# Attention branch: U of the seven-product quads summed ahead, and a fourth such quad in its first pass

## The chip, the cores and the metric

The kernel runs on one core of one Trainium2 chip. The metric is the device time of one execution in microseconds (us), lower is better. A core has a matrix engine (TensorE, "PE"; its weight loads are "PEld"), a vector engine (VectorE, "DVE"), a scalar engine (ScalarE, "ACT"), GpSimd ("POOL") and SyncE ("SP"), which here issues nearly all DMAs. Each engine works through its own instructions in a fixed order; semaphores make them wait for one another.

## The reference

One layer of a hybrid block, batch 1, 256 tokens, width 2048, fp32: causal attention with ALiBi and three dilated patterns (16 heads of 128), a chunked state-space scan (inner width 4096, 8 groups), two sigmoid gates, an output product and norms. Cut to the part around the change:

```python
hn = rms_norm(x, norm_w)
proj = hn @ w_in          # q, k, v, z_a, z_s, xbc, dt, g_a, g_s
...
o_a = o_a.reshape(b, s, ATTN_WIDTH) * jax.nn.silu(z_a)
...
merged = jax.nn.sigmoid(g_a) * (o_a @ w_attn_branch) + jax.nn.sigmoid(g_s) * (y @ w_ssm_branch)
return x + merged @ w_out
```

The change is in `o_a @ w_attn_branch`: 256x2048 by 2048x2048.

## The kernel before

**Precision.** Every fp32 operand is split in a high part h (an ACT copy to the fast fp32 format) and a low part l (a DVE subtract, operand minus h). A product is a "triple" of three matmuls, each 128x128 by 128x512: x-high by h, x-high by l, x-low by h (L484 to L486).

**Stages.** first, dt, the groups B, C, xs, zs (with gs between), then ssm, v, the 16 heads (q, k, za for each), ga, attn, out. All weights lie packed in DRAM as `wall`, tiles of 128x1024 (512 KB), numbered in the order of use: a *unit* is one such tile. attn's first pass has the tiles 417 to 432 and its second 433 to 448. A plain tile is loaded in a ring "w" of 5 places and split to h and l (L278, L279), rings of 4 places each.

**gemm_pair.** ssm, v, ga, attn and out are computed in two passes, c = 0 and c = 2, each over two blocks of 512 columns and both blocks of 128 rows: four accumulators `ps_<stage><c>_0..3`. A pass goes over *quads* of two k-tiles (two weight tiles). In a plain quad all eight products are computed: 24 matmuls. The quads in S_QUADS use a seven-product scheme (Strassen's in Winograd's form): 21 matmuls, with four more accumulators `pp_<stage><c>_0..3`. With the weights as A = (B11, B21), tile n, and (B12, B22), tile n+1, it needs T = (B12 − B11, B22 − B12 + B11), U = A minus T's second half T2, and C = B22. All of A, C, T, U are split: ha/la, hc/lc, htt/ltt, htu/ltu (ACT L551, DVE L552); U is a DVE subtract of 128x1024 (L565), made in place in `wa`. The left sides `sx` are made before. The T and U pairs share two places, ht/lt.

After a pass, *fold* (two ACT copies L589 and L590, four DVE adds L591 to L594) puts the product sums together; in attn, *attend* adds each accumulator (L1154), and *merge* (L1143, L1144) applies the gate to `th_a` and adds to `th_s`. In pass c = 2 accumulators and product banks swap the PSUM banks that they have in c = 0.

**Sums ahead.** For the quads in SUMS_SSM and SUMS_ATT, T is made in an earlier stage, where DVE has time: *sum_jobs* hangs on a unit a `get`, which loads tile n+1 whole and the left half of tile n, and three units later an `add`: two DVE subtracts of 128x512 (L254, L255), then the T is written to DRAM ("spill", L242). A POOL copy of one column (L249, L253) ties each place to the unit. gemm_pair then fetches T (L533) and C (L534) and makes no T. The 21 jobs for ga, attn and out run in the heads' stage, one every 15/4 units, in the space that `th_a` takes up later. In attn, T and C go to `fin`.

**What sets the order.** SP issues loads in the order of the code, each after its place is free. On PE, DVE and ACT a scheduler sets a fixed order when the program is built, by its own estimates of time and the priorities in the code (`high_priority`); the order of quads is written by hand in A_ORDERS.

Of the kernel before, what the change touches and what calls it, by code (L numbers as in the profile page):

```python
# [9 lines left out]
F32 = mybir.dt.float32  # L10
F32R = mybir.dt.float32r
AF = mybir.ActivationFunctionType
ALU = mybir.AluOpType
PSUM = bass.MemoryType.PSUM

P = 128
# [8 lines left out]
UNIT = 1024  # L25
# [12 lines left out]
GT_LAGS = (3, 5, 6), (2, 3, 4)  # L38
Y_AFTER = 0, 0
GS_BEFORE = {0: (0, 1), 4: (2,)}  # L40
A_ORDERS = {0: (0, 1, 2, 4, 3, 6, 5, 7), 2: (0, 2, 1, 4, 3, 5, 6, 7)}
V_ORDERS = {0: (0, 2, 4, 1, 3, 5, 6, 7), 2: (0, 2, 1, 4, 3, 5, 6, 7)}
G_ORDERS = {c: (0, 2, 4, 1, 3, 5, 6, 7) for c in (0, 2)}
O_LEFT = {0: {0: (0, 3), 4: (1, 5)}, 2: {}}
# [5 lines left out]
S_QUADS = {  # L50
    ("ssm", 0): (5, 7, 8, 10, 11, 12, 13), ("ssm", 2): (3, 5, 7, 8, 10, 11, 12, 13),
    ("v", 0): (2, 3, 4, 5, 6), ("v", 2): (2, 4, 5, 6), ("ga", 0): (2, 3, 4, 5, 6), ("ga", 2): (2, 3, 4, 5, 6),
    ("attn", 0): (2, 4, 6), ("attn", 2): (2, 4, 5, 6), ("out", 0): (3, 5), ("out", 2): (3, 5),
}
Y_ORDERS = {0: (0, 1, 2, 3, 5, 4, 7, 8, 6, 10, 11, 9, 12, 14, 13, 15), 2: (0, 3, 1, 5, 2, 7, 8, 4, 10, 11, 6, 12, 9, 13, 14, 15)}
Y_LATE = {12: 4, 13: 6}
SX_Y = sorted({*S_QUADS[("ssm", 0)], *S_QUADS[("ssm", 2)]}, key=Y_ORDERS[0].index)
Y_SPARE = {q: int(q in S_QUADS[("ssm", 0)] and q in S_QUADS[("ssm", 2)]) for q in SX_Y}
SX_X = (2, 4, 3, 5, 6)
O_BEHIND = 3, 14, 15, 17  # L60
SUMS_ATT = [(t, q) for t in [(n, c) for n in ("ga", "attn", "out") for c in (0, 2)] for q in S_QUADS[t]]
ATT_QUADS = sorted({*S_QUADS[("attn", 0)], *S_QUADS[("attn", 2)]})
IN_PLACE = {"ssm": [(0, 12), (2, 12)]}
SUMS_SSM = [(t, q) for t in (("ssm", 0), ("ssm", 2), ("v", 0), ("v", 2)) for q in S_QUADS[t] if (t[1], q) not in IN_PLACE.get(t[0], ())]
# [2 lines left out]
SUM_LAG = 3  # L67
# [131 lines left out]
def hybrid_block(ctx: ExitStack, tc: tile.TileContext, wall, xt, x, pk_d, cst_d, fw_d, out):  # L199
    nc = tc.nc  # L200
    ve, ac, gp, pe = nc.vector, nc.scalar, nc.gpsimd, nc.tensor
# [26 lines left out]

    loaded = {}
    on_unit = {}  # L230
    presum, lefts = {}, {}
    ssm_pool = []

    def behind_unit(n, f):
        on_unit.setdefault(n, []).append(f)
# [4 lines left out]
    def spill(kept, key, name, src, shape):  # L240
        kept[key] = dram.tile([P, *shape], F32, name=name, tag=name)
        nc.sync.dma_start(kept[key], src)  # L242

    def sum_jobs(jobs, units, places):

        def get(tag, q, t, b11, behind):
            n = FIRST[tag] + 2 * q
            for dst, src in ((t, wall[n + 1]), (b11, wall[n, :, :512])):
                gp.tensor_copy(dst[:, 0:1], behind)  # L249
                nc.sync.dma_start(dst, src)  # L250

        def add(tag, q, t, b11, res, behind):
            gp.tensor_copy(res[:, 0:1], behind)  # L253
            ve.tensor_tensor(res[:, :512], t[:, :512], b11, ALU.subtract)  # L254
            ve.tensor_tensor(res[:, 512:], t[:, 512:], res[:, :512], ALU.subtract)  # L255
            spill(presum, (tag, q), f"t_{tag[0]}{tag[1]}_{q}", res, [UNIT])

        for n, ((tag, q), u) in enumerate(zip(jobs, units)):
            t, b11, res = places[n % len(places)]
            behind_unit(u, lambda behind, a=(tag, q, t, b11): get(*a, behind))  # L260
            behind_unit(u + SUM_LAG, lambda behind, a=(tag, q, t, b11, res): add(*a, behind))

    def load(n, cuts=(0, UNIT)):
        if n not in loaded:
# [204 lines left out]
    def gemm_pair(tag, x_of, n_kt, sxs, swap, extra={}, close=1, order=None, room={}, tail=None):  # L469
# [22 lines left out]
        for at, q in enumerate(order):  # L492
            tick()
            for f in extra.get(q, ()):
                f()
            ks = [x_of(2 * q + k) for k in range(2)]
            a = [[(x[:, i * P : (i + 1) * P], x[:, S + i * P : S + (i + 1) * P]) for x in ks] for i in range(2)]
            n = first + 2 * q
            if q not in quads:
                ready = [] if at <= n_q - close else ready  # L500
                ready += [(a, k, *unit(n + k, (2, 512))) for k in range(2)]
                if n_q - close <= at < n_q - 1:
                    continue
                steps = [(e, i, c) for e in ready for i in range(2) for c in range(2)]
                if at == n_q - 1:
                    steps.sort(key=lambda s: s[1:])
                jobs = [(e, i, c, es[2 * i + c], WHOLE, at == 0 and e[1] == 0, e is ready[-1]) for e, i, c in steps]
                if tail and at == n_q - 1:
                    es.append(tail(prods))
                    _, i, c = steps[-1]  # L510
                    jobs = jobs[:-3]
                    for acc, cs in ((es[3][:, LEFT], LEFT), (es[4][:, LEFT], RIGHT)):
                        for n, e in enumerate(ready[-3:]):
                            jobs.append((e, i, c, acc, cs, cs is RIGHT and n == 0, n == 2))
                for (ae, k, h, l), i, c, acc, cs, start, stop in jobs:
                    triple(acc, *ae[i][k], h[:, c, cs], l[:, c, cs], start=start, stop=stop and at == n_q - 1)
                continue
            if not prods:
                prods = banks(p_tags, "pp")
            made = (tag, q) in presum  # L520

            def place(kind):
                if not room.get(kind):
                    t = ring(f"{kind}{n}")
                    return t[:, 512:] if kind == "wc" else t
                seats[kind] = seats.get(kind, -1) + 1
                return room[kind][seats[kind] % len(room[kind])]

            wa = ring(f"wa{n}")
            nc.sync.dma_start(wa, wall[n])  # L530
            if made:
                wt, wc = place("wt"), place("wc")
                nc.sync.dma_start(wt, presum[tag, q])  # L533
                nc.sync.dma_start(wc, wall[n + 1, :, 512:])  # L534
            else:
                wt = ring(f"wb{n}")
                wc = wt[:, 512:]
                nc.sync.dma_start(wt, wall[n + 1])

            def hl(where, suffix, tags, bufs):  # L540
                return [
                    where.tile([P, UNIT], F32R, name=f"{t}{suffix}{n}", tag=t, bufs=bufs) for t in tags
                ]

            def pair_of(suffix):
                sets = room.get("tl", ())
                seats["tl"] = (seats.get("tl", -1) + 1) % (2 + len(sets))
                return sets[seats["tl"] - 2] if seats["tl"] > 1 else hl(mul, suffix, ("ht", "lt"), 2)

            def part(src, h, l):  # L550
                ac.activation(h, src, AF.Copy)  # L551
                ve.tensor_tensor(l, src, h.bitcast(F32), ALU.subtract)  # L552

            two = lambda t: t.rearrange("p (k m) -> p k m", k=2)
            with tc.high_priority(L_AHEAD):
                if not made:
                    ve.tensor_tensor(wt[:, :512], wt[:, :512], wa[:, :512], ALU.subtract)
                ha, la = hl(stream, "a", "hl", H_BUFS)
                part(wa, ha, la)
                hc, lc = hl(stream, "c", "hl", H_BUFS)  # L560
                part(wc, hc[:, :512], lc[:, :512])
                if not made:
                    ve.tensor_tensor(wt[:, 512:], wt[:, 512:], wt[:, :512], ALU.subtract)
                t2 = wt[:, 512:].unsqueeze(1).to_broadcast([P, 2, 512])
                ve.tensor_tensor(two(wa), two(wa), t2, ALU.subtract)  # L565
                ht, lt = pair_of("t")
                part(wt, ht, lt)
                hu, lu = pair_of("u")
                part(wa, hu, lu)
            sx = sxs[q]  # L570
            lo, hi = slice(0, 512), slice(512, 1024)
            go, end = q == seven[0], q == seven[-1]
            for acc, x, h, l, cs, own in (
                (prods[0], a[0][0], ha, la, lo, True),
                (es[0], a[0][1], ha, la, hi, False),
                (es[1], sx[3], hc, lc, lo, False),
                (prods[1], sx[0], ht, lt, lo, True),
                (prods[2], sx[2], ht, lt, hi, True),
                (prods[3], sx[1], hu, lu, lo, True),
                (es[2], a[1][1], hu, lu, hi, False),  # L580
            ):
                triple(acc, *x, h[:, cs], l[:, cs], start=(own and go), stop=(own and end))
# [109 lines left out]
    with tc.tile_pool(name="ssm", bufs=2) as sp:  # L692
# [212 lines left out]
        for c in GS_BEFORE[0]:  # L905
# [4 lines left out]
        begin = FIRST[("xs", 4)]  # L910
        sum_jobs(
            SUMS_SSM, [FIRST[("B", g)] + n for g in range(1, 7) for n in SUM_UNITS],
            [(sums_at[:, 0], sums_at[:, 2, :512], sums_at[:, 1])],
        )

        def left_x(q, behind):
# [127 lines left out]
    with tc.tile_pool(name="att", bufs=2) as ap:  # L1044
# [33 lines left out]
        def mix(h, pT, za):  # L1078
# [10 lines left out]
            if h % 2 == 1 and q in ATT_QUADS:  # L1089
# [1 line left out]

        sum_jobs(
            SUMS_ATT, [FIRST[("q", 0)] + 3 + n * 15 // 4 for n in range(len(SUMS_ATT))],
            [
                (th_a[:, i, :UNIT], th_a[:, 1, UNIT + 512 * i : UNIT + 512 * i + 512], th_a[:, 0, UNIT:])
                for i in range(2)
            ],
        )

        for h in range(NH):  # L1100
# [25 lines left out]

    with tc.tile_pool(name="fin", bufs=2) as fp:
        fin = big.tile([P, 2, D], F32, name="fin", tag="yo1a")
        room = {"wt": [fin[:, i, UNIT:] for i in range(2)], "wc": [fin[:, i, :512] for i in range(2)]}

        def turn_m(c, pair, b):
            tp = bank(b, 4 if b == "g" else 2, f"mtp{c}{pair}")
# [150 lines left out]
```

## Time and profile before

| | |
|---|---|
| time of three runs | 1382.22, 1381.36, 1379.6 us; median 1381.36 |
| the profiled execution | 1379.87 us; its span on the core 1378.0, so 1.9 lie around the span |
| granted PE clock | 0.998 |
| DMA of queue 1 (hardware) | 340.67 MB, 74.0% of 16 engines |
| attn in the trace | about 1202 to 1285 us |

A span is the time from the first to the last instruction on the core. In the profile, a row of a timeline gives the start, the duration, the engine, the line, the operation, and out<-in by the tiles' names without their numbers (`ps_attn` is any of the attn accumulators); brackets at the end tell how long the engine stood idle before and what ended that. A row of a list by line gives the number of instructions, then shortest/median/longest duration in ns, then the first and the last start.

### The profile page before, as it was taken

What the parts mean: (1) busy time and instruction counts of PE and PEld (TensorE: products, weight loads), DVE (VectorE), ACT (ScalarE), POOL (GpSimd) and SP (SyncE); (2) the same over time, 40 slices, a digit from 0 to 9 for tenths busy, and PEclk for the clock granted to TensorE, in tenths of its full rate; (3) what the DMA queues carried; (4) which work ended last, traced back from release to release, by engine and by line L of the source; (5) the groups of instructions that cost most, each with busy time, mean ns of one, the idle gap of its engine ahead of it and who ended that gap; (6) DMA issues with size and microseconds to landing.
All of it is one profiled execution on the core that took longest, in us unless ns stands there. A gap on an engine that the chain in (4) does not pass through costs nothing.

```text
span 1378.0 us, 20734 instructions
## 1 busy us (share of the span) xinstructions
PE 1366.8 (99%) x7260; PEld 1164.8 (85%) x7260; DVE 1177.0 (85%) x1763; ACT 840.0 (61%) x1310; POOL 161.7 (12%) x238
## 2 busy tenths in 40 slices
PE   9999999999999999999999999999999999999997
PEld 7888888888888888888888888888888888888886
DVE  6898899898899888788989888777877789988897
ACT  7655777675667676666565554454444557655564
POOL 2301211101020100010001001211211000400112
PEclk9999999999999999999999999999999999999999
DMA  9767878778787867578677568888889757875773
GB/s 342 237 190 237 298 267 286 262 244 288 248 277 237 298 203 220 174 242 277 228 261 270 211 215 316 306 275 280 306 298 302 230 163 267 291 244 173 246 273 122
DMA packets 106520, 348.15 MB, mean 253 GB/s; under 512 B 11888, under 2 KB 14256, under 8 KB 106416
## 3 DMA queue, kind: packets, MB, share of 16 engines
q1 hardware_dynamic: 104400, 340.67, 74.0%
q10 hardware_dynamic: 1440, 4.06, 0.8%
q0 software_dynamic: 576, 2.10, 0.4%
q8 instruction: 57, 0.93, 0.3%
q14 instruction: 47, 0.39, 0.1%
HBM read 316.97 MB, written 29.82 MB: 252 GB/s over the span
## 4 chain that ended last, share of the span: by engine, by line
PE 98%; DMA 0%; DVE 0%; ACT 0%; issue 0%; SPq 0%; POOL 0%; POOLq 0%; DVEq 0%
PE ps_xs L333 8%; PE ps_zs L333 8%; PE ps_k L333 4%; PE ps_za L333 4%; PE ps_q L333 4%; PE ps_zs L339 4%; PE ps_xs L339 4%; PE ps_ssm L485 3%; PE ps_ssm L486 3%; PE ps_ssm L484 3%; PE ps_q L339 2%; PE ps_za L339 2%; PE ps_k L339 2%; PE ps_gs L421 2%; PE ps_gs L422 2%; PE ps_gs L420 2%
## 5 line engine op out<-in xcount | busy, mean ns | idle before, releaser
L278 ACT ACTIVATE h<-w 128x1024 fp32r<-128x1024 f32 (+1 forms) x394 | 410.0, 1048 | 306.0 <-issue 73.7
L279 DVE TENSOR_TENSOR l<-w,h 128x1024 fp32r<-128x1024 f32 (+1 forms) x394 | 474.0, 1209 | 111.1 <-ACT h L278 106.9
L333 PE MATMUL ps_zs<-XT,h 128*128 128x512 f32 x496 | 172.0, 393 | 0.0
L333 PE MATMUL ps_xs<-XT,h 128*128 128x512 f32 x496 | 171.6, 393 | 0.0
L339 PE MATMUL ps_zs<-XT,l 128*128 128x256 f32 x496 | 134.6, 279 | 0.0
L339 PE MATMUL ps_xs<-XT,l 128*128 128x256 f32 x496 | 133.7, 277 | 0.0
L333 PEld LDWEIGHTS ps_xs<-XT,h 128*128 128x128 f32 x496 | 91.3, 188 | 19.4
L333 PEld LDWEIGHTS ps_zs<-XT,h 128*128 128x128 f32 x496 | 91.3, 188 | 18.9
L339 PEld LDWEIGHTS ps_zs<-XT,l 128*128 128x128 f32 x496 | 93.3, 188 | 2.1
L339 PEld LDWEIGHTS ps_xs<-XT,l 128*128 128x128 f32 x496 | 93.2, 188 | 2.1
L333 PE MATMUL ps_q<-XT,h 128*128 128x512 f32 x256 | 91.1, 404 | 0.0
L333 PE MATMUL ps_k<-XT,h 128*128 128x512 f32 x256 | 88.6, 395 | 0.0
L333 PE MATMUL ps_za<-XT,h 128*128 128x512 f32 x256 | 88.4, 394 | 0.0
L551 ACT ACTIVATE ha<-wa 128x1024 fp32r<-128x1024 f32 x45 | 47.5, 1056 | 45.9 <-PE ps_ssm L486 10.0
L339 PE MATMUL ps_q<-XT,l 128*128 128x256 f32 x256 | 68.4, 278 | 0.0
L339 PE MATMUL ps_k<-XT,l 128*128 128x256 f32 x256 | 68.4, 277 | 0.0
L339 PE MATMUL ps_za<-XT,l 128*128 128x256 f32 x256 | 68.4, 277 | 0.0
L552 DVE TENSOR_TENSOR la<-wa,ha 128x1024 fp32r<-128x1024 f32 x45 | 54.8, 1218 | 8.4 <-ACT ha L551 8.3
L552 DVE TENSOR_TENSOR ltu<-wa,htu 128x1024 fp32r<-128x1024 f32 x40 | 48.7, 1219 | 10.8 <-ACT htu L551 10.8
L793 ACT ACTIVATE gt<-acb,acT 128x128 f32<-128x128 f32 x128 | 44.1, 390 | 22.2 <-DMA acb<-acum_d 21.9
L333 PEld LDWEIGHTS ps_k<-XT,h 128*128 128x128 f32 x256 | 47.0, 188 | 9.9
L333 PEld LDWEIGHTS ps_q<-XT,h 128*128 128x128 f32 x256 | 47.1, 188 | 9.7
(691 smaller groups left out, 3347.8 us busy)
## 6 DMA issues: line engine op xcount, KB each, us to landing
w<-in_wall SPq DMA_DIRECT2D x390, 512.0 KB, 4.8
wa<-in_wall SPq DMA_DIRECT2D x45, 512.0 KB, 4.7
th_a<-in_wall SPq DMA_DIRECT2D x21, 512.0 KB, 4.7
sums_at<-in_wall SPq DMA_DIRECT2D x18, 512.0 KB, 5.0
acb<-acum_d SPq DMA_DIRECT2D x32, 256.0 KB, 3.8
t_ssm<-sums_at SPq DMA_DIRECT2D x13, 512.0 KB, 4.3
wt<-t_ssm SPq DMA_DIRECT2D x13, 512.0 KB, 4.7
th_a<-in_wall SPq DMA_DIRECT2D x21, 256.0 KB, 5.4
```

The source lines that it names most:

```text
L278: ac.activation(h[:, a:b], w[:, a:b], AF.Copy)
L279: ve.tensor_tensor(l[:, a:b], w[:, a:b], h[:, a:b].bitcast(F32), ALU.subtract)
L333: high = pe.matmul(acc, h[:, kk, :], xs_of(kt), start=(kt == 0), stop=False)
L339: low = pe.matmul(acc[:, S:], l[:, kk, :], xs_of(kt)[:, :S], start=False, stop=(kt == KT - 1))
L420: pe.matmul(accs[i], xh, h[:, kk], start=(kt == 0), stop=False)
L421: pe.matmul(accs[i], xh, l[:, kk], start=False, stop=False)
L484: pe.matmul(acc, xh, h, start=start, stop=False)
L485: pe.matmul(acc, xh, l, start=False, stop=False)
L486: pe.matmul(acc, xl, h, start=False, stop=stop)
L551: ac.activation(h, src, AF.Copy)
L552: ve.tensor_tensor(l, src, h.bitcast(F32), ALU.subtract)
L793: ac.activation(g4[:, n, b], acb[:, j, b // 2 * P : b // 2 * P + P], AF.Relu, scale=-1.0, bias=sc[:, h : h + 1],)
```

## The change

Four edits. (1) For attn's seven-product quads 2, 4, 5, 6 of both passes, `add` also makes U, in place of the loaded tile n (now loaded whole), and spills it; gemm_pair fetches it ("wu"), to a place of its own (`room_u`) and to the ring by turns, and has no U subtract there. (2) Quad 5 of attn's first pass becomes a seven-product quad, so SUMS_ATT has 22 jobs, and the order of that pass is 0, 1, 2, 4, 5, 6, 3, 7. (3) T is made in place, without a result tile; the two places of the heads' stage are a T tile and a whole tile each, and the earlier sums of ssm and v have two places for one. (4) A place may be given as None, for the ring.

```diff
-A_ORDERS = {0: (0, 1, 2, 4, 3, 6, 5, 7), 2: (0, 2, 1, 4, 3, 5, 6, 7)}
+A_ORDERS = {0: (0, 1, 2, 4, 5, 6, 3, 7), 2: (0, 2, 1, 4, 3, 5, 6, 7)}
...
-    ("attn", 0): (2, 4, 6), ("attn", 2): (2, 4, 5, 6), ("out", 0): (3, 5), ("out", 2): (3, 5),
+    ("attn", 0): (2, 4, 5, 6), ("attn", 2): (2, 4, 5, 6), ("out", 0): (3, 5), ("out", 2): (3, 5),
...
+U_QUADS = 2, 4, 5, 6
...
+SUMS_U = {(t, q) for t, q in SUMS_ATT if t[0] == "attn" and q in U_QUADS}
...
-        def get(tag, q, t, b11, behind):
+        def get(tag, q, t, b, behind):
             n = FIRST[tag] + 2 * q
-            for dst, src in ((t, wall[n + 1]), (b11, wall[n, :, :512])):
+            b = b if (tag, q) in SUMS_U else b[:, :512]
+            for dst, src in ((t, wall[n + 1]), (b, wall[n, :, : b.shape[-1]])):
                 gp.tensor_copy(dst[:, 0:1], behind)
                 nc.sync.dma_start(dst, src)
-        def add(tag, q, t, b11, res, behind):
-            gp.tensor_copy(res[:, 0:1], behind)
-            ve.tensor_tensor(res[:, :512], t[:, :512], b11, ALU.subtract)
-            ve.tensor_tensor(res[:, 512:], t[:, 512:], res[:, :512], ALU.subtract)
-            spill(presum, (tag, q), f"t_{tag[0]}{tag[1]}_{q}", res, [UNIT])
+        def add(tag, q, t, b, behind):
+            name = f"{tag[0]}{tag[1]}_{q}"
+            ve.tensor_tensor(t[:, :512], t[:, :512], b[:, :512], ALU.subtract)
+            ve.tensor_tensor(t[:, 512:], t[:, 512:], t[:, :512], ALU.subtract)
+            spill(presum, (tag, q), f"t_{name}", t, [UNIT])
+            if (tag, q) in SUMS_U:
+                t2 = t[:, 512:].unsqueeze(1).to_broadcast([P, 2, 512])
+                two = b.rearrange("p (k m) -> p k m", k=2)
+                ve.tensor_tensor(two, two, t2, ALU.subtract)
+                spill(u_sums, (tag, q), f"u_{name}", b, [UNIT])
...
+            if (tag, q) in u_sums:
+                wu = place("wu")
+                nc.sync.dma_start(wu, u_sums[tag, q])
...
-                t2 = wt[:, 512:].unsqueeze(1).to_broadcast([P, 2, 512])
-                ve.tensor_tensor(two(wa), two(wa), t2, ALU.subtract)
+                if (tag, q) not in u_sums:
+                    wu = wa
+                    t2 = wt[:, 512:].unsqueeze(1).to_broadcast([P, 2, 512])
+                    ve.tensor_tensor(two(wa), two(wa), t2, ALU.subtract)
                 ht, lt = pair_of("t")
                 part(wt, ht, lt)
                 hu, lu = pair_of("u")
-                part(wa, hu, lu)
+                part(wu, hu, lu)
...
-            [(sums_at[:, 0], sums_at[:, 2, :512], sums_at[:, 1])],
+            [(sums_at[:, n], sums_at[:, 2, n * 512 : n * 512 + 512]) for n in range(2)],
...
-            [
-                (th_a[:, i, :UNIT], th_a[:, 1, UNIT + 512 * i : UNIT + 512 * i + 512], th_a[:, 0, UNIT:])
-                for i in range(2)
-            ],
+            [(th_a[:, i, :UNIT], th_a[:, i, UNIT:]) for i in range(2)],
...
-        room = {"wt": [fin[:, i, UNIT:] for i in range(2)], "wc": [fin[:, i, :512] for i in range(2)]}
+        room = {
+            "wt": [fin[:, i, UNIT:] for i in range(2)], "wc": [fin[:, i, :512] for i in range(2)],
+            "wu": [fp.tile([P, UNIT], F32, name="room_u", tag="room_u", bufs=1), None],
+        }
```

The lines move: in the changed kernel the matmuls are L492 to L494, the splits of plain tiles L286 and L287, those of the sevens L564 and L565, fold L604 to L609, the add of attend L1169, merge L1158 and L1159.

How the change moves instructions, at two places. The first is PE at the end of attn's first pass. Tiles: 423 and 424 are quad 3, 427 and 428 quad 5, 429 and 430 quad 6, 431 and 432 quad 7; 433 is the first of the second pass. Before, the last matmuls on quad 6's U stand here, 39 rows ahead of the second pass:

```order
L484 MATMUL ps_attn0_3_12302<-h428_12552,oaTb_10585 128x512
L485 MATMUL pp_attn0_3_12381<-ltu429_12520,sx_o6_12315 128x512
L486 MATMUL pp_attn0_3_12381<-htu429_12519,sx_o6_12315 128x512
L485 MATMUL ps_attn0_2_12301<-ltu429_12520,oaTb_10585 128x512
L486 MATMUL ps_attn0_2_12301<-htu429_12519,oaTb_10585 128x512
L484 MATMUL ps_attn0_2_12301<-h427_12546,oaTb_10585 128x512
```

Now, the last on pp_attn0_2, pp_attn0_3, on quad 6's U, and the first of those behind them:

```order
L494 MATMUL pp_attn0_2_12374<-htt429_12517,sx_o6_12309 128x512
L492 MATMUL ps_attn0_2_12295<-htu429_12521,oaTb_10569 128x512
L493 MATMUL pp_attn0_3_12375<-ltu429_12522,sx_o6_12309 128x512
L494 MATMUL pp_attn0_3_12375<-htu429_12521,sx_o6_12309 128x512
L493 MATMUL ps_attn0_2_12295<-ltu429_12522,oaTb_10569 128x512
L494 MATMUL ps_attn0_2_12295<-htu429_12521,oaTb_10569 128x512
L492 MATMUL ps_attn0_2_12295<-h423_12548,oaTa_8466 128x512
L493 MATMUL ps_attn0_2_12295<-l423_12549,oaTa_8466 128x512
L494 MATMUL ps_attn0_2_12295<-h423_12548,oaTa_8466 128x512
```

Nine more on ps_attn0_2 follow (tiles 424, 431, 432, three each), then four on h433, one for each accumulator of the second pass, and then the first on l433. So the last row of pp_attn0_2 stands 18 rows ahead of the second pass, that of pp_attn0_3 15, that of htu429 13 and that of h423 10.

The second place is DVE at the same boundary. Before:

```order
L279 TENSOR_TENSOR l431_12583<-w431_12580,h431_12582 128x1024
L591 TENSOR_TENSOR fin_12298<-pp_attn0_2_12380,fin_12298 128x512
L279 TENSOR_TENSOR l432_12589<-w432_12586,h432_12588 128x1024
L552 TENSOR_TENSOR ltt437_12721<-fin_12298,htt437_12720 128x1024
L592 TENSOR_TENSOR fin_12298<-pp_attn0_3_12381,fin_12298 128x512
L593 TENSOR_TENSOR fin_12298<-fin_12298 128x512
L279 TENSOR_TENSOR l433_12670<-w433_12667,h433_12669 128x1024
L594 TENSOR_TENSOR fin_12298<-fin_12298 128x512
L279 TENSOR_TENSOR l434_12676<-w434_12673,h434_12675 128x1024
L1154 TENSOR_TENSOR fin_12298<-ps_attn0_0_12299,fin_12298 128x512
```

Now:

```order
L287 TENSOR_TENSOR l432_12591<-w432_12588,h432_12590 128x1024
L565 TENSOR_TENSOR ltt429_12518<-fin_12291,htt429_12517 128x1024
L565 TENSOR_TENSOR ltu429_12522<-wu429_12507,htu429_12521 128x1024
L606 TENSOR_TENSOR fin_12291<-pp_attn0_2_12374,fin_12291 128x512
L607 TENSOR_TENSOR fin_12291<-pp_attn0_3_12375,fin_12291 128x512
L1169 TENSOR_TENSOR fin_12291<-ps_attn0_0_12293,fin_12291 128x512
L565 TENSOR_TENSOR ltt437_12723<-fin_12291,htt437_12722 128x1024
L608 TENSOR_TENSOR fin_12291<-fin_12291 128x512
L1158 SCALAR_TENSOR_TENSOR th_a_7784<-th_a_7784,fin_12291 128x512
L565 TENSOR_TENSOR ltu437_12727<-room_u_12292,htu437_12726 128x1024
L287 TENSOR_TENSOR l433_12672<-w433_12669,h433_12671 128x1024
L609 TENSOR_TENSOR fin_12291<-fin_12291 128x512
```

Fold, a first add and a merge of the first pass, and both splits of quad 2's T and U of the second pass, stand ahead of l433 now; before, three fold adds and one of these splits did, with two splits of quad 7 among them. On ACT the order there is now htt437, htu437, h433, h434; each takes over a place that quad 6's T, quad 6's U, quad 3's h423 and h424 leave.

More of the change, by code (lines that the diff above doesn't have):

```diff
@@ L230, in hybrid_block @@
     on_unit = {}
-    presum, lefts = {}, {}
+    presum, u_sums, lefts = {}, {}, {}
     ssm_pool = []
@@ L244, in sum_jobs @@
     def sum_jobs(jobs, units, places):
-        def get(tag, q, t, b11, behind):
+        def get(tag, q, t, b, behind):
             n = FIRST[tag] + 2 * q
-            for dst, src in ((t, wall[n + 1]), (b11, wall[n, :, :512])):
+            b = b if (tag, q) in SUMS_U else b[:, :512]
+            for dst, src in ((t, wall[n + 1]), (b, wall[n, :, : b.shape[-1]])):
                 gp.tensor_copy(dst[:, 0:1], behind)
                 nc.sync.dma_start(dst, src)
-        def add(tag, q, t, b11, res, behind):
-            gp.tensor_copy(res[:, 0:1], behind)
-            ve.tensor_tensor(res[:, :512], t[:, :512], b11, ALU.subtract)
-            ve.tensor_tensor(res[:, 512:], t[:, 512:], res[:, :512], ALU.subtract)
-            spill(presum, (tag, q), f"t_{tag[0]}{tag[1]}_{q}", res, [UNIT])
+        def add(tag, q, t, b, behind):
[8 more added lines that the diff above has]
+                spill(u_sums, (tag, q), f"u_{name}", b, [UNIT])
         for n, ((tag, q), u) in enumerate(zip(jobs, units)):
-            t, b11, res = places[n % len(places)]
-            behind_unit(u, lambda behind, a=(tag, q, t, b11): get(*a, behind))
-            behind_unit(u + SUM_LAG, lambda behind, a=(tag, q, t, b11, res): add(*a, behind))
+            t, b = places[n % len(places)]
+            behind_unit(u, lambda behind, a=(tag, q, t, b): get(*a, behind))
+            behind_unit(u + SUM_LAG, lambda behind, a=(tag, q, t, b): add(*a, behind))
     def load(n, cuts=(0, UNIT)):
@@ L522, in place @@
             def place(kind):
-                if not room.get(kind):
+                seats[kind] = seats.get(kind, -1) + 1
+                spots = room.get(kind) or [None]
+                t = spots[seats[kind] % len(spots)]
+                if t is None:
                     t = ring(f"{kind}{n}")
                     return t[:, 512:] if kind == "wc" else t
-                seats[kind] = seats.get(kind, -1) + 1
-                return room[kind][seats[kind] % len(room[kind])]
+                return t
             wa = ring(f"wa{n}")
```

## The prediction

> **What bounds the kernel now.** I read the page first (busy shares, the chain that ended last), then the waits of TensorE (PE), then windows by stage, then the timelines around the one place where the change reorders work.
>
> ```profile
> PE 1366.8 (99%) x7260; PEld 1164.8 (85%) x7260; DVE 1177.0 (85%) x1763; ACT 840.0 (61%) x1310; POOL 161.7 (12%) x238
> PE 98%; DMA 0%; DVE 0%; ACT 0%; issue 0%; SPq 0%; POOL 0%; POOLq 0%; DVEq 0%
> ```
> ```profile
> engine line waited for: us in total, times, longest us
> PE warm L630 <- DVE ssq L627: 1.4, 1, 1.4
> PE ps_first L385 <- ACT h L278: 1.4, 2, 1.1
> ```
>
> The first row is busy time by engine, the second the chain. PE is busy for 99% of the span and is 98% of the chain; its list of waits holds two entries, both in the first stage. So after the start nothing that VectorE (DVE), ScalarE (ACT) or a DMA does is waited for: time goes only if PE has fewer matmuls, and comes only if PE begins to wait.
>
> ```profile
> core 0: us, PE busy (x) PEld busy (x) DVE busy (x) ACT busy (x) POOL busy (x), PEclk, DMA share, GB/s
> 838.00:1117.00 279.00, 279.00 (x1632) 245.33 (x1631) 209.40 (x406) 137.39 (x215) 40.75 (x58) 1.00 0.83 278
> 1202.00:1243.00 41.00, 41.00 (x182) 33.94 (x182) 37.18 (x43) 24.03 (x28) 0.00 (x0) 1.00 0.71 237
> 1243.00:1285.00 42.00, 42.00 (x195) 34.82 (x194) 37.30 (x46) 25.07 (x32) 3.16 (x1) 1.00 0.60 192
> ```
>
> The windows are the stage of the heads (q, k, za), where the new sums are made, and the two passes of attn. In attn the DVE is busy for 37 of 41 us. It is close to PE there, though not ahead of it: cover is thin wherever DVE work must fall between two matmuls.
>
> **The PE term.** The end of attn's first pass and the start of its second:
>
> ```profile
> 1240.12 0.39 PE L485 MATMUL ps_attn<-l,oaTb 128*128 128x512 f32 x1
> 1240.35 0.39 PE L486 MATMUL ps_attn<-h,oaTb 128*128 128x512 f32 x1
> 1240.57 0.39 PE L484 MATMUL ps_attn<-h,oaTa 128*128 128x512 f32 x1
> 1240.80 0.39 PE L485 MATMUL ps_attn<-l,oaTa 128*128 128x512 f32 x1
> ```
>
> Starts are 0.2265 us apart (0.23, 0.22, 0.23); the 0.39 is the time to a result. Quad 5 goes from 8 products of 3 matmuls to 7: 24 − 21 = 3 matmuls, 3 × 0.2265 = **−0.68 us**. Without a wait, the second pass would begin at 1240.57 − 0.68 = 1239.89.
>
> **The DVE and ACT terms of attn.**
>
> ```profile
> L565 DVE TENSOR_TENSOR wa<-wa,fin x7: 1214/1217/1218, 1208.1 to 1273.7; 128x1024 f32<-128x1024 f32 x7
> L552 DVE TENSOR_TENSOR lc<-fin,hc x7: 680/683/693, 1207.5 to 1271.6; 128x512 fp32r<-128x512 f32 x7
> L551 ACT ACTIVATE htt<-fin x7: 1044/1061/1067, 1196.6 to 1272.1; 128x1024 fp32r<-128x1024 f32 x7
> ```
>
> Seven U subtracts go: 7 × 1.217 = 8.5 us of DVE. Quad 5 as a seven has three 1024-wide splits and one of 512 in place of two of 1024: + 1.22 + 0.68 = 1.9 us of DVE. Net −6.6 us in 83, beside PE work, worth nothing in itself: no row shows PE waiting for it. On ACT quad 5 adds 1.06 + 0.62 = 1.7 us beside 25 of 42 us busy: nothing.
>
> **The order at the boundary.** In the old order quad 6, the last seven, is followed by two whole plain quads, 5 and 7. Rows of before, PE and then DVE:
>
> ```profile
> 1231.51 0.39 PE L485 MATMUL pp_attn<-ltu,sx_o 128*128 128x512 f32 x1
> 1231.73 0.39 PE L486 MATMUL pp_attn<-htu,sx_o 128*128 128x512 f32 x1
> ```
> ```profile
> 1230.50 1.22 DVE L279 TENSOR_TENSOR l<-w,h 128x1024 fp32r<-128x1024 f32 x1
> 1231.63 1.22 DVE L552 TENSOR_TENSOR ltt<-fin,htt 128x1024 fp32r<-128x1024 f32 x1
> 1232.77 0.68 DVE L592 TENSOR_TENSOR fin<-pp_attn,fin 128x512 f32<-128x512 f32 x1
> 1233.49 0.69 DVE L593 TENSOR_TENSOR fin<-fin 128x512 f32<-128x512 f32 x1
> 1234.38 1.23 DVE L279 TENSOR_TENSOR l<-w,h 128x1024 fp32r<-128x1024 f32 x1 [0.21 <-ACT h L278]
> 1235.53 0.68 DVE L594 TENSOR_TENSOR fin<-fin 128x512 f32<-128x512 f32 x1
> 1236.43 1.22 DVE L279 TENSOR_TENSOR l<-w,h 128x1024 fp32r<-128x1024 f32 x1 [0.22 <-ACT h L278]
> 1237.57 1.28 DVE L1154 TENSOR_TENSOR fin<-ps_attn,fin 128x512 f32<-128x512 f32 x2
> 1238.77 1.28 DVE L1143 SCALAR_TENSOR_TENSOR th_a<-th_a,fin 128x512 f32<-128x512 f32 x2
> ```
>
> The last product bank is done at 1231.73, 39 matmuls ahead of the boundary. l433, the low part that the second pass needs first, is made at 1234.38 and used at 1240.80: 5.2 us in hand, with most of the merge behind it. Back to back, a 1024-wide instruction holds the DVE 1.13 us (1230.50 to 1231.63) and a 512-wide one 0.60 us (two from 1237.57 to 1238.77).
>
> In the changed order the T and U products of quad 6 come last but for 12 matmuls. Counting back from 1239.89 at 0.2265 a row, plus 0.39 to the result: pp_attn0_2 is complete at 1236.20 (18 rows before), pp_attn0_3 at 1236.88 (15), the slot of htu429 is free at 1237.34 (13), that of h423, which h433 takes, at 1238.01 (10).
>
> ACT: htt437 1236.20 to 1237.26, htu437 1237.34 to 1238.40, h433 1238.40 to 1239.46: in time for 1239.89, by 0.4.
>
> DVE, in its new order: first fold add 1236.20, second 1236.88, the add of ps_attn0_0 1237.48, ltt437 1238.08, third fold add 1239.21, merge 1239.81, ltu437 1240.41, l433 1241.54, done at 1242.76. PE has four matmuls on h433 and then wants l433, at 1239.89 + 4 × 0.2265 = 1240.80. It waits **1.96 us**. Put otherwise: after pp_attn0_2 the DVE has five instructions of 0.60, three of 1.13 (the last ending after 1.22) and a wait of 0.08, 6.56 us in all, and PE has 22 matmuls less the 0.39, 4.6 us.
>
> Behind l433 stand l434 (done 1245.09; wanted 12 matmuls after l433, at 1245.48), and then merge work between l435 and l436: ten instructions of 0.60 and four of 1.13 bring l436 to 1253.3, where 45 matmuls and four transposes bring PE to it at 1253.3 too. So nothing more, or 0.3 us. The bounds of this term: if results came a spacing after the start (0.23 in place of 0.39) it is 1.8; if DVE work found some gap I don't see it is 0, which is the lower end, since a matmul cannot run before its operand; above, a slip at the second boundary as large again, 3.9. I take 1.96, since its pieces are all rows of these instructions.
>
> **The sums made ahead.** In the heads' stage each of 8 jobs gains a U subtract (1.22, by the L565 row) and one job more its two 512-wide subtracts (2 × 0.69): 8 × 1.22 + 1.4 = 11.1 us of DVE where 279 − 209.4 = 69.6 is idle: cost nothing. POOL loses 39 copies of 12% busy time: nothing.
>
> Their DMA is the uncertain cost. Per U: 0.26 MB more read (a whole 128x1024 tile for its half) and 0.52 written.
>
> ```profile
> 950.00:1041.00 91.00, 91.00 (x534) 80.07 (x533) 69.91 (x138) 45.38 (x71) 16.88 (x25) 1.00 0.86 293
> 1060.00:1070.00 10.00, 10.00 (x60) 8.81 (x59) 7.52 (x16) 5.40 (x10) 0.31 (x1) 1.00 1.00 355
> GB/s 117 303 393 322 205 203 139 388 399 351 297 342 322 281 220 110 268 400 375 398 270 257 363 411 272 301 337 340 221 227 195 228 344 414 301 220 274 337 366 194
> w<-in_wall SPq DMA_DIRECT2D x30, 512.0 KB, 5.4
>   ACT h L278: 1.0, 1
> 999.90 1.06 ACT L278 ACTIVATE h<-w 128x1024 fp32r<-128x1024 f32 x1 [1.72 <-PE ps_k L333]
> ```
>
> One w is loaded per unit: 30 in the 91 us from 950 to 1041 (fourth row) make a unit 3.03 us, and a job, every 3.75 units, 11.4. The eight attn jobs lie in about these 91 us. 8 × 0.786 = 6.3 MB in 91 us make 293 + 69 = 362 GB/s. The share of 0.86 at 293 would be 341 GB/s at full share; one window at share 1.00 carried 355, and slices of 2.3 us (third row) up to 411. By 341 the loads fall behind by 21 GB/s × 91 us = 1.9 MB, 5.6 us; by 400 not at all. Against that stands a lead: ACT splits w as soon as PE frees one of four h slots (last row), some three units or 9 us ahead, and a late w held h up once, for 1.0 us (fifth row, from the list of who waited for w). So I take **0**, with ends 0 and 5.6.
>
> A rule speaks against the change here. The Trainium skill, "HBM Reference", Specifications (TRN2), gives about 358 GB/s as a core's share, and says that a core streaming alone measures well above it. The 355 at share 1.00 agrees with the share, the slices at 399 to 414 with the second half. By 358 the stage would fall behind by 4 GB/s × 91 us, 0.4 MB or 1 us, which the lead hides; by the sentence on a core alone, not at all.
>
> Attn itself then fetches 8 U tiles, and for quad 5 T and C in place of a plain tile: 237 and 192 GB/s rise by 4.5 MB in 83 us, 54 GB/s. At 291 it stays below the heads' stage today: nothing. U alternates between its own tile and the ring, so no load waits for the tile just being read.
>
> **Sum.** −0.68 + 1.96 + 0 = +1.3 us: the profiled execution's 1379.87 becomes 1381.2. It lies 1.5 below the median of the three runs; on the median, 1381.36 + 1.3 = **1382.6**.
>
> **The rivals.** *No new wait* (0.17): l433 comes in time and only the three matmuls count, 1380.7. It takes 2 us less DVE work in front of l433 than the order shows; nothing in the rows gives it, but the sum hangs on one boundary. *A second wait* (0.14): as much again where the second pass hands over to the out stage, or at l434 to l436; +3.3, 1384.6. It decides if DVE reaches these splits 0.4 us later than I count. Slower than what can be told. *The DMA* (0.11): past 341 GB/s the lead is used up, up to 5.6 more, 1388.2. It decides when w lands more than some 9 us late. *The U tiles save nothing and the plain cost remains* is no separate case, since PE does not see the subtract. Something that makes it faster by over 0.2% (0.04): no row offers more than 0.68 us on PE, so this is for what I have overlooked; the runs alone differ by 2.6 us.
>
> **Chances.** The forecast, 0 to +2.7, has 0.54. A measurement of this kernel tells about 0.2%, 2.8 us, from no change. Within it lie the forecast and the first rival: 0.71. Slower are the second wait and the DMA: 0.25. Faster 0.04. The range runs from the first rival less half the runs' spread either way (1380.7 − 0.9 = 1379.8) to most of the DMA case, 1386.8; what is left out above is some 0.06 and below about as much.
>
> **What would show it.** Right: a wait of PE for l at L287 of about 2 us at the start of the second attn pass, the only new one of its size; 3 fewer matmuls; no L565 subtract on fin, replaced by 8 in the heads' stage with DVE busy there up 11 us; DMA share there near 0.95 and no wait of PE in it. Wrong: PE's list of waits as short as before and the span 0.7 down; waits of h for w in 950 to 1060 that reach PE; or a wait for l at the start of the out stage.

## The result, and the profile after

The changed kernel takes 1403.04 us (median of 5 runs, 1402.0 to 1403.66), beside 1381.36 for the kernel before (5 runs): a ratio of 1.0161, interval 1.0149 to 1.0172 (the two medians alone give 1.0157). It is slower by 22 us, where 1382.6 was forecast and 1386.8 was the end of the range. The page of the profiled execution, busy time and chain:

```profile
PE 1374.7 (98%) x7257; PEld 1167.7 (83%) x7257; DVE 1174.9 (84%) x1768; ACT 839.8 (60%) x1312; POOL 104.2 (7%) x201
PE 86%; DVE 4%; DMA 4%; issue 3%; ACT 1%; POOL 0%; SPq 0%; POOLq 0%; DVEq 0%; ACTq 0%
```

PE is no longer 98% of the chain but 86%. DVE has 4% and a DMA 4%, where both had nothing. What PE waited for:

```profile
engine line waited for: us in total, times, longest us
PE ps_xs L347 <- DVE l L287: 3.8, 3, 1.6
PE ptp L1090 <- DVE p L1085: 2.9, 1, 2.9
PE xtp L828 <- DVE xs L413: 2.2, 2, 1.3
PE ps_attn L493 <- DVE l L287: 2.0, 1, 2.0
PE sps L1066 <- DVE kT L401: 1.9, 1, 1.9
...
PE ps_gs L429 <- DVE l L287: 1.3, 1, 1.3
PE ps_zs L347 <- DVE l L287: 1.0, 1, 1.0
PE ps_za L347 <- DVE l L287: 0.8, 1, 0.8
```

One row, ps_attn, is the wait that was forecast, and it is as long as forecast. All other new rows lie far from attn: in the groups B, C, xs, zs, gs, which hold no U at all, and in the heads' stage (ptp, sps, za). In each PE waits for DVE. So the next view is what DVE waited for, of the changed kernel:

```profile
DVE l L287 <- ACT h L286: 59.8, 76, 2.1
DVE th_a L257 <- DMA th_a<-in_wall: 47.1, 19, 5.1
DVE sums_at L257 <- DMA sums_at<-in_wall: 36.6, 13, 5.5
```

and of the kernel before, on the same subtract:

```profile
DVE th_a L254 <- POOL th_a L253: 3.5, 3, 1.5
DVE th_a L254 <- DMA th_a<-in_wall: 1.0, 1, 1.0
```

L257 is the first subtract of a sum made ahead. The DVE now stands there for 83.7 us in all until the loads land, up to 5.5 us at a time. Before, it stood 1.2 us for these loads (1.0 on th_a and 0.2 on sums_at), and 3.5 for the GpSimd copy that the change dropped. DVE works in order, so everything behind the subtract stands too. One such place, rows of DVE and then of PE:

```profile
997.09 0.29 DVE L467 TENSOR_TENSOR sxt_o<-sxt_o 128x128 f32<-128x128 f32 x1
999.22 0.69 DVE L257 TENSOR_TENSOR th_a<-th_a 128x512 f32<-128x512 f32 x1 [1.84 <-DMA th_a<-in_wall]
999.83 0.28 DVE L468 TENSOR_TENSOR sxt_o<-sxt_o 128x128 f32<-128x128 f32 x1
1000.03 1.22 DVE L287 TENSOR_TENSOR l<-w,h 128x1024 fp32r<-128x1024 f32 x1
```
```profile
1001.30 0.39 PE L347 MATMUL ps_za<-XT,l 128*128 128x256 f32 x1 [0.77 <-DVE l L287]
```

DVE has work but waits 1.84 us for th_a. Two rows later comes l, done at 1001.25, and PE starts on it at 1001.30 after a wait of 0.77.

Where the time went, by the first matmul of a stage (before: ps_q at 821.71, ps_ga at 1116.45, the last bank ps_right at 1368.44 us; after: 833.06, 1138.39, 1392.80): +11.4 us up to the heads, +10.6 in the heads' stage, +2.4 from ga to the end. Of the 11.4, the list above holds 8.3 us of waits (xs, xtp, gs, zs).

### The profile page after: what moved, and what is told of

Its sections match the earlier page's. It is cut to its first block, busy times and chain, and to the rows that moved or that the text cites. A ratio compares the mean times of both kernels' runs of the same rounds, so it can differ in the third digit from the quotient of the medians.

```text
span 1401.9 us, 20693 instructions
## 1 busy us (share of the span) xinstructions
PE 1374.7 (98%) x7257; PEld 1167.7 (83%) x7257; DVE 1174.9 (84%) x1768; ACT 839.8 (60%) x1312; POOL 104.2 (7%) x201
## 4 chain that ended last, share of the span: by engine, by line
PE 86%; DVE 4%; DMA 4%; issue 3%; ACT 1%; POOL 0%; SPq 0%; POOLq 0%; DVEq 0%; ACTq 0%
PE ps_xs L341 7%; PE ps_zs L341 7%; PE ps_q L341 4%; PE ps_k L341 4%; PE ps_za L341 4%; PE ps_zs L347 3%; PE ps_xs L347 3%; PE ps_ssm L493 3%; PE ps_ssm L494 3%; PE ps_ssm L492 3%; PE ps_q L347 2%; PE ps_k L347 2%; PE ps_za L347 2%; PE ps_gs L429 2%; PE ps_gs L430 2%
## 5 line engine op out<-in xcount | busy, mean ns | idle before, releaser
L286 ACT ACTIVATE h<-w 128x1024 fp32r<-128x1024 f32 (+1 forms) x392 | 406.5, 1046 | 242.9 <-issue 52.2
L287 DVE TENSOR_TENSOR l<-w,h 128x1024 fp32r<-128x1024 f32 (+1 forms) x392 | 471.8, 1210 | 63.1 <-ACT h L286 59.8
L341 PEld LDWEIGHTS ps_zs<-XT,h 128*128 128x128 f32 x496 | 91.2, 187 | 18.6
L341 PE MATMUL ps_q<-XT,h 128*128 128x512 f32 x256 | 94.0, 414 | 0.0
L564 ACT ACTIVATE ha<-wa 128x1024 fp32r<-128x1024 f32 x46 | 48.6, 1056 | 50.5 <-DMA wa<-in_wall 10.9
L565 DVE TENSOR_TENSOR la<-wa,ha 128x1024 fp32r<-128x1024 f32 x46 | 56.2, 1221 | 12.5 <-ACT ha L564 11.6
L341 PEld LDWEIGHTS ps_za<-XT,h 128*128 128x128 f32 x256 | 46.9, 188 | 9.8
```

The source lines that it names most:

```text
L286: ac.activation(h[:, a:b], w[:, a:b], AF.Copy)
L287: ve.tensor_tensor(l[:, a:b], w[:, a:b], h[:, a:b].bitcast(F32), ALU.subtract)
L341: high = pe.matmul(acc, h[:, kk, :], xs_of(kt), start=(kt == 0), stop=False)
```

## The experiments

The suspicion: in the old `add` the copy of one column into the result tile did not only cost GpSimd time. It read h of the unit three after the loads, and wrote where the subtract writes; so the subtract could not be placed ahead of that unit. Without it the scheduler is free to set the subtract earlier, presumably where its own estimate has the loads landed; that estimate was not looked at. Theory 1 is this lost tie. Theory 2 is the DMA traffic of U, theory 3 the new places themselves.

The units whose l stands just ahead of the first subtract of each sum in DVE's order, first nine jobs:

```
before, e1         42 49 56 62 69 76 82 89 96
changed, e2, e3    42 48 54 60 67 74 80 87 94
```

**e1_tie**: the whole change, with a tie that leaves the data as they are.

```diff
...
-            ve.tensor_tensor(t[:, :512], t[:, :512], b[:, :512], ALU.subtract)
+            gp.tensor_scalar(tie, behind, 0.0, None, ALU.mult)
+            ve.scalar_tensor_tensor(t[:, :512], t[:, :512], tie, b[:, :512], ALU.add, ALU.subtract)
...
```

`tie` is a column of zeros, made from h of the unit three after the loads; the subtract adds it.

> The whole change, with one thing given back: the first subtract of each sum made ahead again waits for the unit three after its loads (a one-column GpSimd multiply of that unit's h by zero, which the subtract adds). In DVE's order the subtracts then stand at the units 42, 49, 57, 64 ... as before the change, not at 42, 48, 54, 60. Theory 1 (the lost tie): nearly all of the DVE's 84 us of waiting for DMA at the sums goes, PE waits in the first stages and in the heads' stage go, what is left is the boundary in attn (about 2 us) less 0.7: 1381.5 to 1384. Theory 2 (the DMA of U): the 10.6 us lost in the heads' stage stay, the 11.5 before ssm go: about 1392. Theory 3 (the places: two for ssm, sums in place): nothing changes: 1402 to 1404.

1390.68 us (5 runs), beside 1380.50 for before on the same chip: ratio 1.0073, 1.0060 to 1.0086. The heads' stage takes 294.74 us, as before to the hundredth, with U made and spilled in it: its whole loss was the tie, which speaks against theory 2. The subtracts stand at the units of before (the third and fourth at 56 and 62, where the expectation has 57 and 64), and DVE's waits at the sums fell from 83.7 us to 2.0. But it is not at 1381.5 to 1384: 7.8 us are still lost up to the heads, most of it at one place, and 4.7 after ga begins. Rows of e1's waits of PE, and windows around the first:

```profile
PE xtp L831 <- DVE xs L416: 3.2, 1, 3.2
PE ps_attn L496 <- DVE l L290: 2.0, 1, 2.0
...
PE pp_ga L495 <- ACT ha L567: 0.6, 1, 0.6
```
```profile
core 0: us, PE busy (x) PEld busy (x) DVE busy (x) ACT busy (x) POOL busy (x), PEclk, DMA share, GB/s
178.00:182.00 4.00, 0.85 (x6) 0.53 (x5) 2.86 (x5) 4.00 (x8) 0.00 (x0) 0.86 0.48 132
182.00:186.00 4.00, 4.00 (x16) 3.61 (x15) 4.00 (x5) 4.00 (x11) 0.00 (x0) 0.50 0.47 133
```

The wait of 3.2 us ends at 181.7, and behind it the granted clock (third number from the end) is 0.50, for some 6 us by windows of 1 us: with the wait about 6 of the 7.8 us. The tie and the old copy read h of the same units. What differs is the order that the scheduler set around them. Rows of ACT at this place, e1 and then before:

```profile
176.30 0.70 ACT L811 ACTIVATE gt<-acb,acT 128x128 f32<-128x128 f32 x2 [2.76 <-DMA acb<-acum_d]
179.28 0.41 ACT L415 ACTIVATE th_x<-cv_x 128x256 f32<-128x256 f32 x1
```
```profile
172.12 0.41 ACT L404 ACTIVATE th_x<-cv_x 128x256 f32<-128x256 f32 x1
173.97 0.70 ACT L793 ACTIVATE gt<-acb,acT 128x128 f32<-128x128 f32 x2 [1.45 <-DMA acb<-acum_d]
```

DVE's xs, for which PE waits, needs th_x. In e1 th_x stands behind the rows that wait for a load (acb); before, it stood ahead of them. Why the scheduler set it so was not tried apart.

**e2_places**: the kernel of before with the new places and without the copy; no U, quad 5 plain, old order.

```diff
-        def add(tag, q, t, b11, res, behind):
-            gp.tensor_copy(res[:, 0:1], behind)
-            ve.tensor_tensor(res[:, :512], t[:, :512], b11, ALU.subtract)
+        def add(tag, q, t, b, behind):
+            ve.tensor_tensor(t[:, :512], t[:, :512], b, ALU.subtract)
...
-            [(sums_at[:, 0], sums_at[:, 2, :512], sums_at[:, 1])],
+            [(sums_at[:, n], sums_at[:, 2, n * 512 : n * 512 + 512]) for n in range(2)],
...
```

> The kernel of before with the new places of the sums alone: T in place, no GpSimd copy ahead of the subtract, two places for ssm. No U ahead, quad 5 plain, old order of attn. Theory 1: nearly the whole loss is here, some 11 us before ssm and 9 to 11 in the heads' stage: 1400 to 1403. Theory 2 (the DMA of U): 11 us before ssm have no U in them, so at most those: 1381 to 1393. Theory 3: 1400 to 1403 as theory 1.

1399.99 us (4 runs), ratio 1.0138, 1.0123 to 1.0154. Nearly the whole loss, with no U in the program: theory 2 falls. Up to the heads +11.4, as in the change; in the heads +8.5.

**e3_nocopy**: the kernel of before without one line.

```diff
-            gp.tensor_copy(res[:, 0:1], behind)
```

> The kernel of before without the GpSimd copy into the result tile, and nothing else: its result tile and its old places stay. Theory 1: the subtracts stand one or two units earlier on DVE, and the time is as with the new places, 1400 to 1403. Theory 3 (the places themselves): as before the change, 1380 to 1382.

1402.86 us (2 runs), ratio 1.0161, 1.0142 to 1.0179: as much as the whole change within the intervals, from one line. Result tile, places, loads and arithmetic are those of before, so theory 3 falls as well. Rows of DVE's waits in e3:

```profile
DVE th_a L253 <- DMA th_a<-in_wall: 57.0, 18, 5.7
...
DVE sums_at L253 <- DMA sums_at<-in_wall: 21.7, 9, 5.7
DVE sums_at L253 <- DMA w<-in_wall: 15.0, 5, 4.2
```

93.7 us of standing at the sums. The loss is 9.1 up to the heads, 13.1 in them, 0.8 behind. The change splits its loss otherwise (11.4, 10.6, 2.4), so that the totals agree so closely is in part chance.

**e4_tie_no_u**: e1 with U made in attn by DVE.

```diff
-SUMS_U = {(t, q) for t, q in SUMS_ATT if t[0] == "attn" and q in U_QUADS}
+SUMS_U = set()
...
```

> As e1 (whole change, tie given back), but U is not summed ahead: attn makes U with its DVE subtract as before; quad 5 stays a seven-product quad and the new order stays. Theory 1: no wait at the sums; at the end of attn's first pass l433 stands ahead of the split of quad 2's U and has one instruction of 1.13 us less in front, so the boundary wait is 0 to 0.3 us and only the three matmuls count: 1380 to 1381.5. If the U tiles are worth something to PE, it is slower than e1.

1388.34 us (5 runs), ratio 1.0054, 1.0041 to 1.0066. A miss on two counts: the wait at 181 us of e1 is here too (4.2 us), and in attn three gaps between the starts of matmuls are too long, by 0.6, 1.0 and 0.4 us, where 0 to 0.3 was expected. To judge U and quad 5, the part before the heads had to be taken out.

**e5_ssm_old**: sums for ssm and v wholly as before the change; tie of e1 for the others; U, quad 5 and the new order as changed.

```diff
...
+            if res is not None:
+                gp.tensor_copy(res[:, 0:1], behind)
+                ve.tensor_tensor(res[:, :512], t[:, :512], b, ALU.subtract)
+            else:
+                res = t
+                gp.tensor_scalar(tie, behind, 0.0, None, ALU.mult)
+                ve.scalar_tensor_tensor(t[:, :512], t[:, :512], tie, b[:, :512], ALU.add, ALU.subtract)
...
+            [(sums_at[:, 0], sums_at[:, 2, :512], sums_at[:, 1])],
...
+            [(th_a[:, i, :UNIT], th_a[:, i, UNIT:], None) for i in range(2)],
...
```

> The sums for ssm and v are made exactly as before the change (result tile, one place, GpSimd copy), so DVE's order up to the heads is that of before; the sums for ga, attn and out are in place with the tie of e1; U ahead, quad 5 and the new order as in the change. Theory 1 (the lost tie, and at 181 us of e1 a chance order of its own): nothing is lost before ssm and in the heads' stage; only attn is left, with the boundary wait of 2.0 to 2.2, three matmuls less, and up to 2 us of waits in ga and of lower clock: 1381.5 to 1385. If the DMA of U costs something in the heads' stage, ga starts later than at 1116.5 by as much.

1382.71 us (11 runs) beside 1380.49 (27 runs): ratio 1.0017, 1.0008 to 1.0026, so +2.2 us. Waits of PE in e5, all of them after the first stage:

```profile
PE ps_attn L501 <- DVE l L295: 2.0, 1, 2.0
...
PE pp_ga L500 <- ACT ha L572: 0.3, 1, 0.3
```

With the dependency in place (the old copy for ssm and v, the tie for the others), the rest of the change costs 2.2 us (interval 1.1 to 3.6); the +1.3 forecast for the whole change lies within that, and the main wait is the one that was forecast.

**e7_no_u**: e5 with the line of e4.

> As e5, but U is made in attn by DVE as before the change; quad 5 and the new order stay. The end of the first pass has l433 in time, but the U subtracts of the second pass come between its splits, where e4 showed three waits, 2.1 us in all: 1381.5 to 1383.5. If U ahead is what costs, it is faster than e5 by over 2; if U ahead pays, slower.

1382.57 us (11 runs), ratio 1.0016, 1.0007 to 1.0025: as e5, so U ahead neither paid nor cost here. Without U ahead the wait of 2.0 us is gone, and three shorter ones (1.2 for l and 0.3 for ltu in the list) take its place in the second pass.

**e8_u_only**: e5 with quad 5 plain and the old order of the first pass.

```diff
-A_ORDERS = {0: (0, 1, 2, 4, 5, 6, 3, 7), 2: (0, 2, 1, 4, 3, 5, 6, 7)}
+A_ORDERS = {0: (0, 1, 2, 4, 3, 6, 5, 7), 2: (0, 2, 1, 4, 3, 5, 6, 7)}
...
-    ("attn", 0): (2, 4, 5, 6), ("attn", 2): (2, 4, 5, 6), ("out", 0): (3, 5), ("out", 2): (3, 5),
+    ("attn", 0): (2, 4, 6), ("attn", 2): (2, 4, 5, 6), ("out", 0): (3, 5), ("out", 2): (3, 5),
...
```

> As e5, but quad 5 of the first pass is plain and the order of that pass is the old one: U ahead alone. l433 then has one T split and two fold adds ahead of it, and some 39 matmuls of cover, so no boundary wait, and no matmul saved: within 1 us of before, whatever DVE saves.

1385.36 us (5 runs), ratio 1.0039, 1.0027 to 1.0052: a miss. The boundary is free, as expected, but the list of waits has three new ones elsewhere:

```profile
PE ps_out L502 <- DVE mT L304: 1.9, 1, 1.9
...
PE pp_attn L500 <- ACT htu L572: 0.8, 1, 0.8
...
PE pp_ga L500 <- ACT ha L572: 0.6, 1, 0.6
```

The relief of DVE (7 subtracts less in attn) is worth nothing here, and the waits that come with the new order cost more. What in the order makes the wait for mT was not tried. The wait for ha in ga is in the lists of e1, e5, e8 and e11, and not in those of e4 and e7, which make U in attn; why it comes with U ahead was not tried either.

**e11_order**: e5 with two other orders of quads.

```diff
-A_ORDERS = {0: (0, 1, 2, 4, 5, 6, 3, 7), 2: (0, 2, 1, 4, 3, 5, 6, 7)}
+A_ORDERS = {0: (0, 2, 4, 1, 5, 6, 3, 7), 2: (0, 1, 2, 4, 3, 5, 6, 7)}
...
```

> As e5 (U ahead, quad 5 a seven), with the orders (0, 2, 4, 1, 5, 6, 3, 7) for the first pass and (0, 1, 2, 4, 3, 5, 6, 7) for the second. The last row on pp_attn0_3 then stands 33 rows ahead of the second pass, 7.1 us, and ahead of l433 the DVE has 4.7 us of work after it: no boundary wait, and only the three matmuls count: 0.7 us faster than before. If a wait for T or U tiles at the start of attn takes its place, slower than that.

1380.48 us (11 runs), ratio 1.0001, 0.9993 to 1.0010: no difference from before. The boundary wait is gone, as reckoned. Of the 0.7 us that three matmuls save none shows, though the interval, −1.0 to +1.4 us, can't exclude it; the list has 0.6 us for ha in ga, which before did not have:

```profile
PE pp_ga L500 <- ACT ha L572: 0.6, 1, 0.6
```

It is the best of these versions that hold the change, and does not beat the kernel before.

## Why the prediction was wrong, step by step

**What bounds the kernel** was right: time came only from new waits of PE.

**The PE term and the boundary** were right. The wait was put at 1.96 us; the profile has 2.0 in the change, in e1 and in e5. The changed kernel's DVE at that place ran the reckoned chain:

```profile
1258.59 0.69 DVE L606 TENSOR_TENSOR fin<-pp_attn,fin 128x512 f32<-128x512 f32 x1 [3.57 <-PE pp_attn L494]
1259.39 0.69 DVE L607 TENSOR_TENSOR fin<-pp_attn,fin 128x512 f32<-128x512 f32 x1
1259.99 0.68 DVE L1169 TENSOR_TENSOR fin<-ps_attn,fin 128x512 f32<-128x512 f32 x1
1260.59 1.22 DVE L565 TENSOR_TENSOR ltt<-fin,htt 128x1024 fp32r<-128x1024 f32 x1
1261.72 0.68 DVE L608 TENSOR_TENSOR fin<-fin 128x512 f32<-128x512 f32 x1
1262.33 0.69 DVE L1158 SCALAR_TENSOR_TENSOR th_a<-th_a,fin 128x512 f32<-128x512 f32 x1
1262.93 1.22 DVE L565 TENSOR_TENSOR ltu<-room_u,htu 128x1024 fp32r<-128x1024 f32 x1
1264.07 1.22 DVE L287 TENSOR_TENSOR l<-w,h 128x1024 fp32r<-128x1024 f32 x1
```

From the first fold add to the start of l433 it is 5.48 us; 5.34 was reckoned. The first row shows the DVE idle for 3.57 us just ahead: it had time, but its work was not there yet, which is why DVE's busy share said nothing of this wait. With the dependency back, in e5, the sum of +1.3 stands beside +2.2, interval 1.1 to 3.6 (1380.49 x 0.0008 and x 0.0026).

**The DMA of U** was right at 0. e5's heads' stage, with the jobs' full traffic, beside before:

```profile
840.00:1120.00 280.00, 280.00 (x1635) 246.07 (x1633) 221.43 (x423) 138.92 (x218) 49.47 (x61) 1.00 0.87 305
```
```profile
840.00:1120.00 280.00, 280.00 (x1634) 246.05 (x1633) 211.25 (x412) 138.66 (x219) 40.75 (x58) 1.00 0.82 277
```

The first is e5, the second before. DVE is busy 10.2 us more (11.1 reckoned), the DMA moves 305 GB/s for 277, and PE is busy for all 280 us in both. In the 91 us from 950 to 1041, for which 362 GB/s were reckoned, e5 moves 354 at a share of 0.97.

**The step that failed** is "POOL loses 39 copies of 12% busy time: nothing". The copy was priced by GpSimd's time. It was also the only thing that held the subtracts behind the third unit, and it was that for the sums of ssm and v too, for which the prediction has no term. e3 takes away this line alone and is 22 us slower. The prediction compares the order of PE and DVE around attn; on DVE, the sums of the groups stand one or two units earlier, as the table above shows, and that it does not compare. The 69.6 us of idle DVE did hide the 11.1 us of added work, as e5 shows, but they were no cover for this: a wait at a DMA uses up idle time and then holds back every split behind it.

The rival of a slow DMA spoke of w landing late. ACT waited 17.9 us in all for w in the result, and 18.6 before, so that is not what happened. In the groups the 512 KB loads of the sums took as long as before (median from issue to landing 5.0 us before, 5.1 after), in the heads' stage longer (4.7 and 6.0); DVE came to them earlier in both. No rival had the change of a dependency in it.

Two numbers of the prediction are wrong without effect on this: half the spread of the three runs is 1.3 us and not 0.9, so the range would begin at 1379.4; and the fastest slice in its row is 414 GB/s, not 411.

What stays open: of the 10.6 us lost in the heads, the list holds 5.6 us of waits (ptp, sps, za), and the lower clock described below accounts for 3.3; the remaining 1.7 are not assigned, nor are some 3 of the 11.4 up to the heads. Most of the 7.8 us that e1 loses up to the heads lies at one place, behind one changed order; what changed that order was not found. The tie alone in the kernel before was not run, so what it costs by itself within e5's 2.2 us is not shown.

## What to carry to other kernels

A copy, a memset or a touch of one column can be there for the dependency that it makes. Before pricing its removal by its engine's time, ask which instruction it holds back and where that would stand without it, above all an instruction that reads a DMA's result on an engine that works in order. And compare the static order of every engine over the whole program, not only around the place that the change is about: the edit that looked like housekeeping carried the time. An engine's idle share tells neither whether its work is there when it is idle, nor what stands behind a wait.

## What the runs showed of the hardware

A wait of PE can cost more than its length. Two places of the changed kernel, windows with the granted clock as third number from the end; the waits end at 965.5 (sps, 1.9 us) and 1007.7 (ptp, 2.9 us):

```profile
960.00:968.00 8.00, 6.14 (x35) 5.22 (x34) 7.82 (x10) 2.94 (x5) 1.86 (x2) 0.93 0.81 291
968.00:976.00 8.00, 8.00 (x41) 6.98 (x40) 2.89 (x9) 1.67 (x3) 0.00 (x0) 0.86 0.76 287
1008.00:1012.00 4.00, 4.00 (x16) 3.45 (x16) 3.54 (x6) 1.21 (x3) 0.00 (x0) 0.59 0.91 342
```

The clock shortfall is 8 x 0.07 + 8 x 0.14 + 4 x 0.41 = 3.3 us. All of it lies behind the waits: by windows of 1 us the clock is 1.00 up to 966 and then 0.50 from 967 to 970, and 0.50 from 1008 to 1011. In e1 a wait of 3.2 us was followed by 0.50.

It is not so each time, and the length of the wait alone does not decide it. At the boundary in attn PE waits 2.0 us for l in e1, in e5 and in the changed kernel. In e1, where the wait ends at 1252.3, the clock falls; in e5, where it ends at 1244.15, and in the changed kernel it stays at 1.00. The first two rows are e1, the third is e5:

```profile
1250.00:1254.00 4.00, 1.98 (x7) 1.35 (x6) 4.00 (x5) 1.23 (x2) 0.00 (x0) 0.83 0.81 261
1254.00:1258.00 4.00, 4.00 (x15) 3.17 (x14) 4.00 (x6) 1.06 (x1) 0.00 (x0) 0.74 0.93 323
1244.00:1248.00 4.00, 3.85 (x17) 3.16 (x18) 4.00 (x6) 1.70 (x2) 0.00 (x0) 1.00 0.89 292
```

The Trainium skill, "TensorE: Matmul & The Clock Gate", section "HAM oscillation — how this bites in real kernels", asks for no idle gap of PE over about 3.4 us. Here gaps of 1.9, 2.0, 2.9 and 3.2 us were followed by a clock of 0.50, so the trace differs: the gap that is safe was shorter in these runs.
